# Neighbourhood attention of a two-layer hybrid encoder in twelve hand-ordered units, with the passage between layers and the first loads reordered

## The chip, the cores and the metric

The kernel runs on one core of a Trainium2 chip. A core has TensorE for matmuls (PE in the profile, its weight loads PEld), VectorE (DVE), ScalarE (ACT), GpSimd (POOL) and SyncE (SP, which here only issues DMA transfers). Each engine works through a queue of its own in a fixed order, and semaphores tie the queues together. The metric is the device time of one launch in microseconds (us), as the median of several runs. Less is better.

## The reference

Two layers over 512 tokens of width 1024, all in float32. The mixer of a layer projects the normalised input once, feeds three groups of heads from it, and adds the result to `x`; then a mixture of 16 experts follows, each of which takes its own best 64 tokens.

```python
def hybrid_layer(x, ...):
    hn = rms_norm(x, norm_mix)
    proj = jnp.einsum('bsd,dc->bsc', hn, w_in)               # 1024 -> 2336 columns
    qa, ka, va, cq, ckv, kr, hc, bc, cc = jnp.split(proj, splits, axis=-1)
    qa, ka = rms_norm(qa by heads, q_norm_a), rms_norm(ka by heads, k_norm_a)
    out_a = neighbourhood_attention(qa, ka, va, rpb)         # A: 6 heads of 64, 8 x 16 window on the 8 x 64 grid
    out_b = mla_attention(q, k, v)                           # B: 6 heads, q 96, v 64, all 512 keys
    out_c = short_conv_mixer(hc, bc, cc, conv_w)             # C: gated convolution of width 3, 256 channels
    mixed = concat(rms_norm(out_a), rms_norm(out_b), rms_norm(out_c))      # 384 + 384 + 256
    x = x + jnp.einsum('bsm,md->bsd', mixed, w_out)
    return x + expert_choice_moe(rms_norm(x, norm_ffn), ...)

def expert_choice_moe(x, ...):
    aff = jax.nn.softmax(x @ w_router + b_router)
    gate, idx = lax.top_k(aff.transpose(0, 2, 1), 64)        # each of 16 experts takes 64 tokens
    hid = silu(xs @ w_gate) * (xs @ w_up)                    # 1024 -> 1024
    ys = (hid @ w_down) * gate
    return zeros.at[idx].add(ys)
```

## The kernel before

Tokens lie on partitions in four blocks of 128 (`NJ` = 4). Matmuls that need float32 accuracy outside the experts are made of two rounded parts, `hi` and `lo`: `mm3` issues the three products hi·hi, lo·hi and hi·lo (its matmuls stand as L166, L167 and L168 in the profile, L178 to L180 after the change). ACT casts the hi part, and POOL or DVE subtracts it for the lo part.

The mixer has five stretches. `latents` loads the first weights by halves of a pair of row blocks (`wchunk`: a DMA, two casts L330 on ACT, two subtractions L331 on POOL), normalises `x` block by block (`norm_in`: Square L297, Ln and Exp L149/L151, a multiplication L300 on DVE, eight transposes L304 on PE, casts L309 and L310), and projects the latents of B (416 columns). `b_prep` and `conv` follow. Then `weave` drives `b_attn` step by step and slips steps of `a_prep`, the projection of A's q, k and v in 384-column pieces, between its steps as fills; `weave` drives `a_attn` in the same way, with loads of the output weights (`wo_loads`, L705, casts L712, subtractions L713) and the output products of C (`o1`, six 512-column matmuls a step) and B (`o2`, nine a step) as fills. The last, `o3`, multiplies A's own part after A's group norm (L381 to L389), and each output product is added to `x` on DVE (L726). In these stretches a scheduler orders each engine's queue from the written order and priorities (`first` gives the main generator a higher one).

`a_attn` goes over three pairs of heads and four query blocks. A head needs 64 rows of the array for its scores: 128 queries against 256 keys (outer blocks) or 384 keys (inner blocks). For each head: three score matmuls into a bank `sc`; the custom reduction TTR on DVE (L669: adds the bias, yields the negated maximum); Exp with its sum on ACT (L671); a reciprocal and a scaling on DVE (L673, L674); transposes into the bank `pt` (L677); a copy of these out of the bank (L679, on DVE for the first head of the pair and on ACT for the second); and the products with v (L685, 64 columns of the array each). The banks are four `prj`, two `sc`, one `pt` and one `po`.

The mixture of experts takes the experts in eight pairs. Its weights stream through nine slots of 2 MB, issued by SP (L892) in the order of use; the slots lie over the mixer's buffers, so the first loads wait until the mixer lets these go. A pair needs twelve loads of 2 MB. Matmuls of the experts are plain float32 (L158, `acc`). The last pair of a layer computes its two output halves one after the other and adds each with `scatter_rows` (cast and residue L958 and L959, products into `wk`, additions L965).

## Time and profile before

| | us |
|---|---|
| median of 3 runs | 1526.09 |
| lowest, highest | 1523.46, 1526.93 |
| the profiled execution | 1528.57 |
| its span | 1526.8 |

| engine | busy us | share of the span |
|---|---|---|
| PE | 1478.1 | 97% |
| PEld | 858.4 | 56% |
| DVE | 536.7 | 35% |
| ACT | 389.2 | 25% |
| POOL | 232.8 | 15% |

Durations are from the profiled execution; its time is 1.8 us over its span and 2.5 us over the median of the runs. The busy share of PE counts a matmul from its start to its modelled end, and neighbours overlap; the distance from one start to the next says more of what a matmul costs. PEclk in the tables by stretch is the granted TensorE clock, 1.00 for 2.4 GHz and 0.50 for 1.2 GHz. In time order: layer 0's mixer up to about 313 us, its experts up to 761 us, layer 1's mixer up to about 1070 us, its experts to the end.

### The profile page before, as it was taken

What the parts mean: (1) busy time and instruction counts of PE and PEld (TensorE: products, weight loads), DVE (VectorE), ACT (ScalarE), POOL (GpSimd) and SP (SyncE); (2) the same over time, 40 slices, a digit from 0 to 9 for tenths busy, and PEclk for the clock granted to TensorE, in tenths of its full rate; (3) what the DMA queues carried; (4) which work ended last, traced back from release to release, by engine and by line L of the source; (5) the groups of instructions that cost most, each with busy time, mean ns of one, the idle gap of its engine ahead of it and who ended that gap; (6) DMA issues with size and microseconds to landing.
All of it is one profiled execution on the core that took longest, in us unless ns stands there. A gap on an engine that the chain in (4) does not pass through costs nothing. (4 is left out here: it accounts for less than half of the span.)

```text
span 1526.8 us, 19989 instructions
## 1 busy us (share of the span) xinstructions
PE 1478.1 (97%) x8030; PEld 858.4 (56%) x8030; DVE 536.7 (35%) x1220; ACT 389.2 (25%) x969; POOL 232.8 (15%) x336
## 2 busy tenths in 40 slices
PE   7999999999999999999899999999999999999997
PEld 6877766645355355444288766666454554455342
DVE  5475456623023022112164654656130222123022
ACT  6465553400000000100164655543000000000001
POOL 3641360300000000000056314402000000000000
PEclk9999999999999999999999999899999999999999
DMA  5312131889999999999832122219899999999997
GB/s 171 88 46 61 30 111 56 340 315 425 420 427 426 428 427 427 428 428 426 351 89 73 50 55 62 70 56 403 311 422 428 427 428 427 428 427 428 426 429 302
DMA packets 58461, 441.72 MB, mean 289 GB/s; under 512 B 5633, under 2 KB 28161, under 8 KB 32769
## 3 DMA queue, kind: packets, MB, share of 16 engines
q1 hardware_dynamic: 56000, 437.04, 70.2%
q10 hardware_dynamic: 2368, 3.41, 0.8%
q8 instruction: 63, 1.03, 0.3%
q14 instruction: 30, 0.24, 0.0%
HBM read 438.33 MB, written 2.10 MB: 288 GB/s over the span
## 5 line engine op out<-in xcount | busy, mean ns | idle before, releaser
L158 PE MATMUL acc<-w,fmix 128*64 128x512 f32 x3072 | 671.8, 594 | 9.6 <-DMA w<-in_w_up_dram 5.0
L158 PEld LDWEIGHTS acc<-w,fmix 128*64 128x64 f32 x3072 | 215.9, 137 | 428.5 <-issue 407.3
L1001 DVE TENSOR_TENSOR tmp<-acc,tmp 128x512 f32<-128x512 f32 x32 | 22.1, 691 | 396.3 <-issue 368.4
L158 PEld LDWEIGHTS wk<-og,fmix 128*128 128x128 f32 x1024 | 121.0, 191 | 25.9 <-issue 22.7
L158 PE MATMUL wk<-og,fmix 128*128 128x128 f32 x1024 | 132.2, 279 | 0.7 <-DVE og L897 0.7
L995 POOL CAST sel<-con 16x128 bf16<-16x128 f32 x16 | 5.0, 316 | 768.0 <-PE wk L158 761.7
L331 POOL TENSOR_TENSOR wring<-fraw,wring 128x384 fp32r<-128x384 f32 (+1 forms) x88 | 91.2, 1045 | 142.0 <-ACT wring L330 136.7
L1000 ACT ACTIVATE tmp<-acc 128x512 f32<-128x512 f32 x32 | 19.0, 597 | 327.5 <-PE acc L158 327.5
L938 DVE SCALAR_TENSOR_TENSOR ys<-acc,stat,ys 128x256 fp32r<-128x256 f32 x56 | 26.8, 478 | 198.7 <-ACT ys L937 198.7
L937 ACT ACTIVATE ys<-acc,stat 128x256 fp32r<-128x256 f32 x56 | 26.6, 475 | 242.8 <-PE acc L158 191.7
L167 PE MATMUL prj<-wring,hn 128*128 128x384 f32 (+1 forms) x224 | 81.4, 363 | 0.0
L166 PE MATMUL prj<-wring,hn 128*128 128x384 f32 (+1 forms) x224 | 80.5, 361 | 0.3 <-ACT wring L330 0.3
L168 PE MATMUL prj<-wring,hn 128*128 128x384 f32 (+1 forms) x224 | 80.0, 357 | 0.1
L1010 ACT COPY fmix<-wk 128x512 f32<-128x512 f32 x32 | 17.4, 589 | 242.9 <-PE wk L161 242.9
L951 DVE TENSOR_TENSOR x<-wk,x 128x512 f32<-128x512 f32 x112 | 72.0, 684 | 2.2
L158 PE MATMUL wk<-ys,osc 128*128 128x256 f32 x448 | 63.8, 290 | 0.0
L907 DVE TENSOR_TENSOR fmix<-wk,pp 128x128 f32<-128x128 f32 (+1 forms) x86 | 30.7, 356 | 81.5 <-PE wk L158 81.5
L158 PEld LDWEIGHTS wk<-ys,osc 128*128 128x128 f32 x448 | 56.2, 191 | 0.0
L330 ACT CAST wring<-fraw 128x384 fp32r<-128x384 f32 (+1 forms) x88 | 44.5, 514 | 40.3 <-PE prj L167 15.7
L168 PEld LDWEIGHTS prj<-wring,hn 128*128 128x128 f32 x224 | 43.4, 194 | 5.4 <-issue 3.9
L166 PEld LDWEIGHTS prj<-wring,hn 128*128 128x128 f32 x224 | 43.6, 195 | 4.8 <-issue 3.0
L167 PEld LDWEIGHTS prj<-wring,hn 128*128 128x128 f32 x224 | 43.5, 194 | 5.0 <-issue 4.0
(272 smaller groups left out, 2004.6 us busy)
## 6 DMA issues: line engine op xcount, KB each, us to landing
w<-in_w_gate_dram SPq DMA_DIRECT2D x64, 2048.0 KB, 22.9
w<-in_w_up_dram SPq DMA_DIRECT2D x64, 2048.0 KB, 26.6
w<-in_w_down_dram SPq DMA_DIRECT2D x56, 2048.0 KB, 21.9
w<-in_w_down_dram SPq DMA_DIRECT2D x16, 1024.0 KB, 24.7
fraw<-in_w_in_dram SPq DMA_DIRECT2D x24, 384.0 KB, 3.2
fraw<-in_w_out_dram SPq DMA_DIRECT2D x16, 512.0 KB, 3.5
fraw<-in_w_in_dram SPq DMA_DIRECT2D x48, 128.0 KB, 2.4
fmix<-in_rpb_dram ACTq DMA_DIRECT2D x16, 144.0 KB, 3.4
```

Of the source, the lines that this page charges most:

```text
L158: return tc.keep_in_program_order(PE.matmul(*a, **k))
L166: PE.matmul(ps, ah, bh, start=first, stop=False)
L167: PE.matmul(ps, al, bh, start=False, stop=False)
L168: PE.matmul(ps, ah, bl, start=False, stop=last)
L330: ACT.copy(hi, raw[:, kk, :])
L331: POOL.tensor_tensor(lo, raw[:, kk, :], f(hi), op=OP.subtract)
L907: DVE.tensor_tensor(xsT[:, k0:k0 + nk, :], pg[:, 0:nk * 128].rearrange("p (k s) -> p k s", k=nk), P("gffn")[:, k0:k0 + nk, None].to_broadc ...
L937: ACT.activation(ys[:, 0:256], yq, AF.Copy, scale=gate)
L938: DVE.scalar_tensor_tensor(ys[:, 256:512], yq, gate, f(ys[:, 0:256]), op0=OP.mult, op1=OP.subtract)
L951: DVE.tensor_tensor(xv, po.rearrange("p (j c) -> p j c", j=2), xv, op=OP.add)
L1000: ACT.activation(hid, G[n], AF.Silu)
L1001: DVE.tensor_tensor(hid, U[n], hid, op=OP.mult)
```

## The change

Four places are edited.

1. A's attention. `a_attn` becomes `a_units`: twelve units (a pair of heads and a query block) of three parts, `scores`, `flips` and `output`, which the end of `mixer` calls in a written order: scores of the next unit, fills, transposes of this unit, fills, its products with v. The score matmuls of the two heads alternate. The matmuls of these parts, the softmax instructions, the copies out of the bank and the casts of the output weights are pinned to the written order (`PEo`, `ACTo`, `DVEo`, the last two from a new helper `Pinned`, whose instructions all stand under its line, L173). Both copies are on ACT now. The transposes go to `prj` banks, the probabilities to the seven buffers of `P`, the first output weights too; the output weights come in halves of 256 KB. B's group norm is woven in by steps. One of the twelve steps of `a_prep` moves from B's attention to A's, and the rest of `o2` from behind the last group norm's first matmul to before it.
2. First loads of layer 0. The norm weights come as one row and are spread over the partitions by two matmuls against ones and two ACT copies; of the constants the 128 columns of the identity come first, the rest after the weights; two of the four lo parts go from POOL to DVE; the normalisation runs one block ahead of the projection, no longer two.
3. Between the layers. `scatter_rows` works in 256-column quarters. Behind the first half's additions ACT sums the squares of that half of `x` into `half`, so that layer 1's `norm_in` squares only the other half and takes `half` as the bias of its Ln. `warm` issues matmuls on constants, two before and six after the second half's products.
4. At the end of the last layer the same quarters.

In the written-out orders below a row is one instruction or a run of equal ones, named by the line, the operation, what it writes and what it reads, and the shape. `sc` are scores, `prj` banks of projections and (after) transposes, `pt` transposes before, `po` the products with v, `P`, `tmf` and `tmp` probabilities and their transposes; `qk_103`, `qk_104` (`qk_102`, `qk_103` before) are A's q and k, `wring` and `hn` the operands of A's projection, `qk_106` and `lat` (`qk_105` and `lat` before) those of the output products.

PE in A's attention, before: the stretch with the second and third block of scores of the first pair of heads.

```order
L677 MATMUL pt<-con,tmf 128x128 x2
L167 MATMUL prj<-wring,hn_101 128x384
L168 MATMUL prj<-wring,hn_99 128x384
L166 MATMUL prj<-wring,hn_99 128x384
L167 MATMUL prj<-wring,hn_101 128x384
L168 MATMUL prj<-wring,hn_99 128x384
L166 MATMUL sc<-qk_103,qk_102 128x256
L167 MATMUL sc<-qk_103,qk_102 128x256
L168 MATMUL sc<-qk_103,qk_102 128x256
L166 MATMUL sc<-qk_103,qk_102 128x384
L166 MATMUL prj<-wring,hn_99 128x384
L167 MATMUL sc<-qk_103,qk_102 128x384
```

PE in A's attention, after: the third and fourth unit.

```order
L159 MATMUL sc<-qk_104,qk_103 128x256 x6
L162 MATMUL prj<-con,P 128x128 x6
L159 MATMUL prj<-qk_106,lat 128x512 x6
L159 MATMUL po<-tmp,fmix 64x128
L159 MATMUL po<-tmf,fmix 64x128
L159 MATMUL po<-tmp,fmix 64x128
L159 MATMUL po<-tmf,fmix 64x128
L159 MATMUL po<-tmp,fmix 64x128
L159 MATMUL po<-tmf,fmix 64x128
L159 MATMUL sc<-qk_104,qk_103 128x256 x6
L159 MATMUL prj<-qk_106,lat 128x512 x6
L162 MATMUL prj<-con,P 128x128 x4
```

Scores, transposes and products, which stood singly among the projection's matmuls, now stand in groups of four to six with the fills between the groups.

ACT in A's attention, before: exponentials (L671), copies of transposes (L679) and casts of output weights (L712) in the first pair of heads.

```order
L671 ACTIVATE tmf_2124,stat1_2127<-tmf_2124,stat1_2125 128x256
L671 ACTIVATE tmf_2147,stat1_2150<-tmf_2147,stat1_2148 128x384
L712 CAST hn0_98<-fraw_104 128x512
L679 COPY tmp_2135<-pt_2132 128x256
L712 CAST hn0_98<-fraw_104 128x512
L671 ACTIVATE tmf_2175,stat1_2178<-tmf_2175,stat1_2176 128x384
L712 CAST hn1_99<-fraw_104 128x512 x2
L671 ACTIVATE tmf_2199,stat1_2202<-tmf_2199,stat1_2200 128x384
```

ACT in A's attention, after: two units in the second pair of heads. The exponentials write `P`, the copies `tmp` and `tmf`.

```order
L173 ACTIVATE P_2324,stat1_2327<-P_2324,stat1_2325 128x256
L173 ACTIVATE P_2332,stat1_2335<-P_2332,stat1_2333 128x256
L173 CAST hn1_100<-fraw_105 128x512 x2
L173 COPY tmp_2357<-prj_2354 128x256
L173 COPY tmf_2362<-prj_2359 128x256
L173 COPY fmix_90<-po_2191 128x512
L173 ACTIVATE P_2381,stat1_2384<-P_2381,stat1_2382 128x384
L173 ACTIVATE P_2389,stat1_2392<-P_2389,stat1_2390 128x384
L173 COPY tmp_2408<-prj_2405 128x256
L173 COPY tmf_2413<-prj_2410 128x256
```

Both copies of a unit now stand behind both exponentials of the unit after it, and in this place also behind two casts of output weights.

ACT at the passage between the layers, before: residue casts (`yh`), layer 1's first weights (`qk2`, `wring`) and the norm of block 0 (`fmix` from `x`).

```order
L958 ACTIVATE yh_5155<-acc_5091,stat1_4989 128x256
L330 CAST qk2_5194<-fmix_89 128x416
L958 ACTIVATE yh_5155<-acc_5091,stat1_4989 128x256
L330 CAST qk2_5194<-fmix_89 128x416
L297 ACTIVATE fmix_89,stat1_5224<-x_67 128x1024
L330 CAST wring_5186<-fraw_5193 128x416
L149 ACTIVATE stat1_5226<-stat1_5224,eps_70 128x1
L330 CAST wring_5186<-fraw_5193 128x416
L151 ACTIVATE stat1_5228<-stat1_5226 128x1
```

ACT at the same place after.

```order
L1025 ACTIVATE ys_5182<-acc_5106,stat1_5004 128x256
L347 CAST qk2_5240<-fmix_90 128x416
L1025 ACTIVATE ys_5185<-acc_5106,stat1_5004 128x256
L347 CAST qk2_5240<-fmix_90 128x416
L311 ACTIVATE fmix_90,stat1_5270<-x_67 128x512
L150 ACTIVATE stat1_5272<-stat1_5270,half_82 128x1
L152 ACTIVATE stat1_5274<-stat1_5272 128x1
L311 ACTIVATE fmix_90,stat1_5292<-x_67 128x512
L347 CAST wring_5232<-fraw_5239 128x416 x4
```

The norm's square is half as wide, and its Ln and Exp stand ahead of the casts of `wring`; the first of two `qk2` casts still stands between the two residue casts.

The diff, cut:

```diff
+            return lambda *a, **k: tc.keep_in_program_order(getattr(self.eng, name)(*a, **k))
...
-        for g, _, _ in fills:
-            for _ in g:
-                pass
+        for g, _, w in fills:
+            if w < 5:
+                for _ in g:
+                    pass
...
-            ACT.activation(xn, x[:, j, :], AF.Square, scale=1.0 / 32.0, accum_out=ms)
-            r = rstd_of(ms, 1)
+            if l:
+                ACT.activation(xn[:, 512:1024], x[:, j, 512:1024], AF.Square, scale=1.0 / 32.0, accum_out=ms)
+                r = rstd_of(ms, 1, eps=half[:, j:j + 1])
...
+                    SP.dma_start(row, gm_in[l:l + 1, :])
+                    for n in range(2):
+                        c_ = slice(n * 512, (n + 1) * 512)
+                        ps = sc()
+                        PE.matmul(ps, ones[0:1, :], row[:, c_], start=True, stop=True)
+                        ACT.copy(gm[:, c_], ps)
...
-                SP.dma_start(con, con_in[:, 0:NCON])
+                SP.dma_start(con[:, 0:128], con_in[:, 0:128])
...
+                             None if kp < 2 else F(4992 + (kp - 2) * 832, 832), POOL if l or kp % 2 else DVE)
...
-            ahead = 2
+            ahead = 2 if l else 1
...
+                    pss = [sc(), sc()]
+                    for a, b in ((0, 0), (1, 0), (0, 1)):
+                        for hh in range(2):
+                            rows = slice(hh * 64, hh * 64 + 64)
+                            PEo.matmul(pss[hh][:, 0:n], qkA(0, a)[rows, hp, j * 128:(j + 1) * 128],
+                                       qkA(1, b)[rows, hp, k0 * 128:k1 * 128], start=a + b == 0, stop=b == 1)
...
+                        p = ptile()
...
+                        ACTo.activation(p[:, 0:n], p[:, 0:n], AF.Exp, bias=nm, scale=-1.0, accum_out=s_)
...
+                        pt = prj()
                         for i in range(k1 - k0):
-                            PE.transpose(pt[:, i * 128:(i + 1) * 128], p[:, i * 128:(i + 1) * 128], ident)
-                        pT = tmp()
-                        (ACT.copy if hh else DVE.tensor_copy)(pT[:, 0:n], pt[:, 0:n])
+                            PEo.transpose(pt[:, i * 128:(i + 1) * 128], ps_[hh][:, i * 128:(i + 1) * 128], ident)
+                        pT = (tmp, ftile)[hh]()
+                        ACTo.copy(pT[:, 0:n], pt[:, 0:n])
...
+                for a in {0: (0,), 1: (), 2: (1, 2)}.get(i, (i,)):
+                    if a < len(ks):
+                        raws.append([fraw(a % 2 * 1024 + n * 512, 512) if a else ptile() for n in range(2)])
+                        for n in range(2):
+                            SP.dma_start(raws[a][n], w_out[l, ks[a] * 128:(ks[a] + 1) * 128, n * 512:(n + 1) * 512])
...
+                        ACTo.copy(hi[:, c_], raws[i - 1][n])
...
+                    (DVEo if PE is PEo else DVE).tensor_tensor(x[:, j, c_], ps, x[:, j, c_], op=OP.add)
...
-        weave(b_attn(), 52, (ap, 1, 1), (norm_later(sc, oC, us[:, 0:512], 6, mixC), 1, 0),
-              (ap, 12 - 1, 1))
+        weave(b_attn(), 52, (ap, 1, 5), (norm_later(sc, oC, us[:, 0:512], 6, mixC), 1, 0), (ap, 11 - 1, 5))
...
-        weave(a_attn(), 40, (wl, 3, 0), (o1, 3, 4),
-              (norm_later(sc, oB, F(0, 512), 3, mixB), 1, 0), (wl, 1, 0), (o1, 5 - 3, 4), (wl, 1, 0), (o1, 4, 4),
-              (wl, 1, 0), (o2, 3, 3), (wl, 1, 0), (o2, 3, 3), (wl, 1, 0), (o2, 3, 3), (wl, 1, 0))
+        nb = norm_later(sc, oB, F(0, 512), 3, mixB, PEo, ACTo, DVEo)
+        todo = [(o1, 2), (nb, 1), (o1, 2), (wl, 0), (nb, 1), (o1, 2), (nb, 1), (o1, 2), (nb, 0), (wl, 0), (o1, 2),
+                (o1, 2), (wl, 0), (o1, 2), (o1, 2), (wl, 0)] + [(o2, 3)] * 3 + [(wl, 0)] + [(o2, 3)] * 3
+        todo += [(o2, 3)] * 2 + [(o1, 0), (o2, 0), (wl, 0)]
...
+        next(wl)
+        units[0][0]()
+        for _ in ap:
+            pass
+        next(wl)
+        units[1][0]()
+        next(wl)
+        for u, (_, flips, output) in enumerate(units):
+            if 0 < u < len(units) - 1:
+                units[u + 1][0]()
+            fill()
+            flips()
+            fill()
+            output()
+        tot = tmp()
+        squares(oA, tot)
+        place = places
+        fill()
+        for g, _ in todo:
+            next(g, None)
+        group_norm(sc, oA, tot, 0, mixA)
...
-            hi, lo = tmpr("yh"), tmpr("yl")
-            for q in range(2):
-                q_ = slice(q * 256, (q + 1) * 256)
-                ACT.activation(hi[:, q_], Y[n][:, q_], AF.Copy, scale=gate)
-                DVE.scalar_tensor_tensor(lo[:, q_], Y[n][:, q_], gate, f(hi[:, q_]), op0=OP.mult, op1=OP.subtract)
+            ys = [parts(Y, gate, 2 * n), parts(Y, gate, 2 * n + 1)]
             c_ = slice(n * 512, (n + 1) * 512)
+            between = l < layers - 1 and n
+            if between:
+                warm(2)
             for j in range(NJ):
                 po = wk()
-                PEo.matmul(po, osc[:, j * 128:(j + 1) * 128], hi, start=True, stop=False)
-                PEo.matmul(po, osc[:, j * 128:(j + 1) * 128], lo, start=False, stop=True)
+                for q in range(2):
+                    ps = po[:, q * 256:(q + 1) * 256]
+                    PEo.matmul(ps, osc[:, j * 128:(j + 1) * 128], ys[q][:, 0:256], start=True, stop=False)
+                    PEo.matmul(ps, osc[:, j * 128:(j + 1) * 128], ys[q][:, 256:512], start=False, stop=True)
                 DVE.tensor_tensor(x[:, j, c_], po, x[:, j, c_], op=OP.add)
+                if l < layers - 1 and n == 0:
+                    ACT.activation(po, x[:, j, c_], AF.Square, scale=1.0 / 32.0, accum_out=half[:, j:j + 1])
...
+        def warm(n):
+            po = wk()
+            for _ in range(n):
+                PEo.matmul(po, order[:, 2, :], order.rearrange("p a b -> p (a b)"), start=True, stop=True)
...
+                warm(6)
+                DVE.tensor_scalar(half, half, eps, None, op0=OP.add)
...
```

## Rows read from the trace of the kernel before

**Rows 1.** Busy time by stretch: us, each engine, granted clock, DMA.

```profile
core 0: us, PE busy (x) PEld busy (x) DVE busy (x) ACT busy (x) POOL busy (x), PEclk, DMA share, GB/s
110.00:188.40 78.40, 76.31 (x425) 55.09 (x425) 41.37 (x92) 45.09 (x114) 18.30 (x20) 0.98 0.16 44
188.40:267.80 79.40, 78.05 (x415) 51.87 (x416) 46.26 (x133) 36.79 (x90) 29.85 (x29) 1.00 0.23 80
942.10:1025.50 83.40, 82.21 (x415) 54.92 (x416) 45.85 (x133) 36.57 (x90) 29.85 (x29) 0.94 0.22 76
```

**Rows 2.** Waits of the queue on SP, whole span.

```profile
SPq L892 <- PE sc L168: 69.9, 2, 35.0
```

**Rows 3.** Chain that ended last, layer 1: start, us, engine, what.

```profile
1421.11 33.92 DMA w<-in_w_down_dram
1455.10 39.95 DMA w<-in_w_up_dram
```

**Rows 4.** PE in order of time, 191 us: start, us, line, what.

```profile
191.15 0.33 PE L166 MATMUL prj<-wring,hn 128*128 128x384 f32 x1
191.32 0.33 PE L167 MATMUL prj<-wring,hn 128*128 128x384 f32 x1
...
191.76 0.38 PE L166 MATMUL sc<-qk,qk 64*128 64x256 f32 x1
192.07 0.44 PE L166 MATMUL prj<-wring,hn 128*128 128x384 f32 x1
192.44 0.38 PE L167 MATMUL sc<-qk,qk 64*128 64x256 f32 x1
```

**Rows 5.** One head alone, then two, and their softmax, from 978 us.

```profile
978.63 0.38 PE L166 MATMUL sc<-qk,qk 64*128 64x256 f32 x1
...
979.17 0.50 PE L166 MATMUL prj<-qk,lat 128*128 128x512 f32 x1
...
979.39 0.42 DVE L669 CUSTOM_DVE_ANT_0 tmf<-sc,P 128x256 f32<-128x256 f32 x1 [0.82 <-PE sc L168]
...
979.86 0.51 ACT L671 ACTIVATE tmf<-tmf,stat 128x256 f32<-128x256 f32 x1
...
980.07 0.45 PE L166 MATMUL sc<-qk,qk 64*128 64x256 f32 x2
...
980.49 0.16 DVE L673 RECIPROCAL stat<-stat 128x1 f32<-128x1 f32 x1 [0.67 <-ACT tmf L671]
...
980.79 0.50 PE L166 MATMUL prj<-qk,lat 128*128 128x512 f32 x1
980.82 0.42 DVE L669 CUSTOM_DVE_ANT_0 tmf<-sc,P 128x256 f32<-128x256 f32 x1 [0.16 <-PE sc L168]
...
981.16 0.35 DVE L674 TENSOR_SCALAR tmf<-tmf,stat 128x256 f32<-128x256 f32 x1
```

**Rows 6.** ACT in A's attention, layer 0: groups, mean ns of one.

```profile
L671 ACT ACTIVATE tmf<-tmf,stat 128x384 f32<-128x384 f32 x12 | 7.4, 616 | 8.7 <-DVE stat L669 7.7 <-DVE tmf L674 0.8
...
L712 ACT CAST hn<-fraw 128x512 fp32r<-128x512 f32 x8 | 4.7, 619 | 2.4 <-DMA fraw<-in_w_out_dram 2.4
...
L679 ACT COPY tmp<-pt 128x256 f32<-128x256 f32 x6 | 2.2, 372 | 5.6 <-PE pt L677 5.6
```

**Rows 7.** DVE in the same stretch.

```profile
L726 DVE TENSOR_TENSOR x<-prj,x 128x512 f32<-128x512 f32 x13 | 8.9, 684 | 3.7 <-PE prj L168 3.7
...
L386 DVE SCALAR_TENSOR_TENSOR fmix<-fmix,pp,tmp 128x512 f32<-128x512 f32 x3 | 2.9, 953 | 0.0
L389 DVE TENSOR_TENSOR lat<-fmix,lat 128x512 fp32r<-128x512 f32 x3 | 2.7, 910 | 0.0
```

**Rows 8.** PE at the first projection of layer 0.

```profile
16.15 1.09 PE L304 MATMUL sc<-con,fmix 128*128 128x128 f32 x4 [4.55 <-DVE fmix L300]
```

**Rows 9.** All engines at the passage between the layers.

```profile
769.71 0.66 PE L304 MATMUL sc<-con,fmix 128*128 128x128 f32 x4 [2.29 <-DVE fmix L300]
...
771.95 0.70 PE L166 MATMUL prj<-wring,hn 128*128 128x416 f32 x1
```

More of the change, by code (lines that the diff above doesn't have):

```diff
@@ L125, in build @@
     gab = fix.tile([128, 2], F32, name="gab")
+    half = fix.tile([128, NJ], F32, name="half")
     def C(name):
@@ L163, in build, with __init__, __getattr__, mm3 @@
     PEo = Ordered()
-    def mm3(ps, ah, al, bh, bl, first, last):
+    class Pinned:
+        def __init__(self, eng):
+            self.eng = eng
+        def __getattr__(self, name):
+            return lambda *a, **k: tc.keep_in_program_order(getattr(self.eng, name)(*a, **k))
+    ACTo, DVEo, POOLo = Pinned(ACT), Pinned(DVE), Pinned(POOL)
+    def mm3(ps, ah, al, bh, bl, first, last, PE=PE):
         PE.matmul(ps, ah, bh, start=first, stop=False)
@@ L313, in mixer, with wchunk @@
         ring = [0]
-        def wchunk(kp, segs, n, home=None, raw=None):
+        def wchunk(kp, segs, n, home=None, raw=None, eng=POOL):
             i = ring[0] % 2
@@ L375, in squares, with group_norm, group_norm_steps @@
                 DVE.tensor_tensor(tot, tot, sq, op=OP.add)
-        def group_norm(bank, o, tot, k0, mix):
+        def group_norm(*args):
+            for _ in group_norm_steps(*args):
+                pass
+        def group_norm_steps(bank, o, tot, k0, mix, PE=PE, ACT=ACT, DVE=DVE):
             n = len(o)
@@ L637, in a_prep, with a_units, unit, scores @@
                 (ACT.copy if j % 2 else DVE.tensor_copy)(va[:, j, :], ps[j][:, 0:384])
-        def a_attn():
-            for hp in range(3):
-                bms = [{}, {}]
-                po = pob()
-                for j in range(NJ):
-                    k0, k1 = KEYS_OF[j]
-                    n = (k1 - k0) * 128
-                    pts = []
+        def a_units():
+            po, bms = [None], [{}, {}]
+            def unit(hp, j):
+                k0, k1 = KEYS_OF[j]
+                n = (k1 - k0) * 128
+                ps_, pts = [], []
+                def scores():
+                    if j == 0:
+                        bms[0], bms[1] = {}, {}
                     for hh in range(2):
                         h = 2 * hp + hh
-                        rows = slice(hh * 64, hh * 64 + 64)
                         if MASK_AT[j] not in bms[hh]:
@@ L684, in a_attn @@
                             h = 2 * hp + hh
-                            PE.matmul(po[hh * 64:hh * 64 + 64, j * 128:(j + 1) * 128],
-                                      va[:, k0 + i, h * DH:(h + 1) * DH], pts[hh][:, i * 128:(i + 1) * 128],
-                                      start=i == 0, stop=i == k1 - k0 - 1)
-                ACT.copy(oA[hp], po)
-            tot = tmp()
-            squares(oA, tot)
-            group_norm(sc, oA, tot, 0, mixA)
+                            PEo.matmul(po[0][hh * 64:hh * 64 + 64, j * 128:(j + 1) * 128],
+                                       va[:, k0 + i, h * DH:(h + 1) * DH], pts[hh][:, i * 128:(i + 1) * 128],
+                                       start=i == 0, stop=i == k1 - k0 - 1)
+                    if j == NJ - 1:
+                        ACTo.copy(oA[hp], po[0])
+                return scores, flips, output
+            return [unit(hp, j) for hp in range(3) for j in range(NJ)]
         mixs = mixA + mixB + mixC
```

74 lines of the change are left out of this document (44 added, 30 removed).

## The prediction

> **What bounds the kernel now.** I read the stretches first, then the chain and the waits of SP, then single instructions. In both stretches of A's attention, from the last product of B's attention to the first matmul of A's group norm, PE is busy for nearly the whole time while DVE, ACT and POOL each have a third of the time or more to spare: 78.05 of 79.40 us in layer 0, 82.21 of 83.40 us in layer 1 [rows 1]. So PE sets the length of these stretches today, and the question is what sets it after the change. Layer 1's stretch is 4.0 us longer for the same 415 matmuls, at a mean granted clock of 0.94 against 1.00; that is 12% of the stretch at 1.2 GHz.
>
> The experts' weights come as fast as DMA brings them: the chain that ended last runs through 33.92 and 39.95 us of transfers [rows 3]. Their first load waits for the last scores of A, 35.0 us of waiting in each of the two layers [rows 2], and the nine slots are full when the experts start. So what A's attention gains or loses shifts the whole rest of the layer, and I carry it to the end at its full size.
>
> **What PE would save.** A single matmul of 384 columns follows its like after 0.17 us (191.15 to 191.32). A projection matmul that stands between two score matmuls takes 0.37 us to the next start (192.07 to 192.44), and a score matmul 0.31 us (191.76 to 192.07) [rows 4]. So each change between 128 rows and 64 costs PE about 0.20 us. In the written order the changes per layer between the last product of B and A's group norm fall from 101 to 38: 63 x 0.20 = 12.6 us. The scores of one head take 0.54 us (978.63 to 979.17), those of two heads side by side 0.72 us (980.07 to 980.79) [rows 5]; two apart would take 1.08. Of the 0.36 us, 0.20 is a change that is already counted; with the wider inner blocks I estimate 0.25 us for each of twelve units, 3.0 us. PE alone would give back 15.6 us per layer, 31 us in all.
>
> **What the new order makes of it.** A unit now passes through a ring of waits. Scores of unit u+1; softmax of its first head and then of its second, since DVE holds the first head's reduction, reciprocal and scaling ahead of the second head's reduction; then, on ACT, the two copies of unit u, which stand behind both exponentials of u+1; then the products of u on PE, and only behind these the scores of u+2. For 256 keys, from the start of the scores: the first reduction at 0.75 us (980.07 to 980.82); its exponential 0.47 us later, its reciprocal at 1.10 us (979.39 to 979.86 and to 980.49), the scaling after 0.16 and for 0.35 us [rows 5]. So the second head's reduction starts 1.65 us behind the first, and its exponential ends at 0.75 + 1.65 + 0.47 + 0.51 = 3.4 us, read out by 3.5. Two copies of 0.372 us [rows 6] end at 4.25, the products after an estimated 0.55: 4.8 us. An inner unit's instructions are longer, 0.616 against 0.51 us for the exponential [rows 6], and in the same way comes to 5.9. With its mixed neighbours the mean of four units is 5.37 us. PE's own work for a unit is about 4.4 us: the stretch of 79.4, less 15.6, and with the moved matmuls below some 73 us, of which 16 lie before the loop and about 4 behind it, over twelve. PE would wait 1 us in every unit. The ring, not PE, then sets the stretch, and this is where the saving goes.
>
> The sum of the stretch, for one layer: 88 projection matmuls of 384 columns x 0.173 and the first scores, 16.0 us until the scores of unit 1. Ten turns of the ring, 53.7 us. In two places a pair of weight casts of 0.62 us [rows 6] stands between the exponentials and the copies: 2.5 us. B's group norm puts 0.95 and 0.91 us [rows 7] on DVE ahead of the next reduction in three units; DVE has some 1.2 us free there, so 0.7 each, 2.1 us. From the last scores: softmax 4.2, the copies and products of two units 3.9, their transposes 0.75, the bank's copy, a square and an addition 1.9, about 10.8 us. Together 85.1 us.
>
> Of the 88 projection matmuls 27 lay before this stretch, in B's attention. PE is busy for 76.31 of 78.40 us there [rows 1], so I credit their 4.7 us in full; the least would be nothing, if B's softmax chain sets that stretch once the cover is thinner. That gives 80.4 us against 79.4 and 83.4: +1.0 in layer 0 and -3.0 in layer 1, whose slow clock I take as gone because the alternating scores before it are. Bounds: -15.6 in each layer if PE still sets the stretch; +4.7 if the credit fails, and beyond that see the third rival.
>
> The 20 matmuls of 512 columns that lay behind the group norm's first matmul (4.6 us, at 0.23) now stand before it. I give nothing for them: the products of A wait for Ln, Exp, 0.95 us of scaling and 0.91 us of residue behind that matmul in any case, and two weight casts (1.24 us) stand ahead of the Ln on ACT. Bounds -4.6 and +1.2.
>
> A rule of the Trainium skill speaks against the change. The reciprocal at 980.49 ends 0.67 us of idle time of DVE, spent on an exponential [rows 5], so DVE waited at the head of its queue. The page TensorE: Matmul & The Clock Gate (its table of specifications) says that ScalarE and VectorE take their queue strictly in order and that only TensorE may pull weight loads forward. By it the ready copies wait behind the exponentials and a unit takes 5.37 us; could ACT take them first, it would be PE's 4.4 us. The trace agrees as far as it shows one such wait.
>
> **The first loads.** Before, PE waits 4.55 us for the second block's norm, whose transposes stand in front of the first block's remaining matmuls [rows 8]. One block ahead, this wait goes, but the projection then runs into its weight parts, which ACT and POOL turn out one by one, and a short gap of about 1.2 us opens behind each of two or three later sets of transposes. Net -1.5 us; bounds -4.5 (all of the wait) and +2 (gaps without the gain). The two broadcasting matmuls and copies lie where PE and ACT wait for the weights.
>
> **The passage.** Block 0's square is half as wide and two weight casts leave the way of its Ln, so I estimate its transposes, at 769.71 before [rows 9], some 1.9 us earlier. But its cast to `hn` now stands behind five weight casts on ACT, and POOL has yet to make their residues; of the 1.9 us the first projection matmul, at 771.95 [rows 9], keeps 0.5. The six warming matmuls fill PE's gap; that first matmul lasts 0.70 us [rows 9], against 0.33 for one of 384 columns [rows 4], and if it and the five behind it start 0.17 us closer, as at 2.4 GHz, this is another 1.0 us. Together -1.5 us; bounds -3 and +1.
>
> **The tail.** The first products of the last half start on one quarter instead of two: about 0.1 us, and in the first halves of both layers 0.2 each: -0.5 us, bounds -1 and 0.
>
> Sum: 1.0 - 3.0 - 1.5 - 1.5 - 0.5 = -5.5 us. Against the profiled execution's 1528.57 us this gives 1523.1; that execution lay 2.5 us over the median, so on the median 1526.09 - 5.5 = 1520.6 us.
>
> **Rivals.** (a) PE still sets the stretch. For it: 98% today. Against it: the order of copies behind exponentials. It gives 2 x -15.6 on A, -3.5 on the rest: 1491 us. (b) Half of it, because the scheduled parts overlap better than my ring (the second head's reduction earlier, products behind one copy): 0.6 us less per unit, 11 units, two layers, -13: 1507 us. (c) Slower, by DVE's pinned queue. The additions to `x` (0.684 us [rows 7], five for three units) stand behind the second head's scaling and ahead of the next unit's first reduction, and each waits for a fill that PE issues late. DVE's own chain in a unit, two softmax halves of 1.65 and 1.14 us of additions behind a reduction at 0.75, ends at 5.2 us, against a need at 5.37 + 0.75. The slack is 0.9 us. From the point where an addition's matmuls end later than that, every turn of the ring grows; at 0.9 us a turn, 22 turns, it is +20 us on my sum: 1540 us. (d) The loads hide everything after the passage, and only layer 0's start and the tail count: 1524 us.
>
> **How the numbers follow.** The forecast has 0.42 and spreads over -10 to +4 around it, (a) 0.11, (b) 0.20, (c) 0.22, (d) 0.05. What a measurement of this kernel tells from no change is 0.2%, 3.05 us: below 1523.0 counts as faster, above 1529.1 as slower. Faster: 0.11 + 0.20 + 0.6 x 0.42 = 0.56. Slower: 0.22 + 0.08 x 0.42 = 0.25. Same: the rest, 0.19. The range runs from 1500, below which lies (a), to 1538, near the middle of (c); it leaves out about 0.2. The likeliest case's own range is 1511 to 1525.
>
> **What would show it.** In the profile after: turns of 4.8 to 5.9 us from scores to scores, with PE idle for about 1 us in each, released by ACT's copies; exponentials before copies with no gap between them; 80 to 81 us from the last product of B to A's group norm, once the 4.7 us shorter stretch of B's attention is taken in; granted clock 1.00 there; no wait of 4.55 us before layer 0's second transposes; the first projection of layer 1 about 1.5 us earlier behind the last expert. The forecast is wrong if PE is busy through the loop, if PE's waits end with an addition or a reduction on DVE, or if the clock falls to 1.2 GHz for whole units.

## The result: slower by 1.4%, and the profile after

| | before | after |
|---|---|---|
| median of 3 runs, us | 1526.09 | 1547.88 |
| lowest, highest, us | 1523.46, 1526.93 | 1545.87, 1548.43 |
| span of the profiled execution, us | 1526.8 | 1546.6 |

After to before is 1.0139, 95% interval 1.0122 to 1.0156. The forecast was 1520.6 us, the range 1500 to 1538: the change went the other way and out of the range.

Where the 19.9 us between the two spans lie, by the starts of the same instructions in both traces (us):

| stretch | layer 0 before | after | layer 1 before | after |
|---|---|---|---|---|
| start (layer 1: last expert matmul) to B's first scores | 97.3 | 98.8 | 92.2 | 90.6 |
| to B's last product | 90.7 | 89.2 | 89.2 | 88.5 |
| to the matmul of A's group norm | 79.9 | 94.0 | 83.9 | 94.0 |
| to the first expert matmul | 47.0 | 47.0 | 47.0 | 46.9 |
| the experts | 445.5 | 444.5 | 445.4 | 444.1 |

The loss is A's attention, some 14 and 10 us, and it reaches the end nearly undiminished: the experts take only about 1 us less each than they took. Busy time by stretch, after, for A's two stretches:

```profile
188.00:282.00 94.00, 81.11 (x467) 61.99 (x463) 43.72 (x124) 42.30 (x107) 34.20 (x35) 0.89 0.18 62
952.60:1046.70 94.10, 81.20 (x467) 61.95 (x463) 43.83 (x124) 42.31 (x107) 34.24 (x35) 0.89 0.17 62
```

Against [rows 1] PE has gone from 98% busy to 86%, and the granted clock from 1.00 and 0.94 to 0.89. Inside the stretch, layer 0's loop in three parts: the first turn of the ring (scores of unit 1 to scores of unit 2), turns 2 to 5, and turns 6 to 10:

```profile
204.50:217.08 12.58, 8.79 (x35) 5.01 (x34) 4.82 (x11) 5.94 (x13) 5.66 (x5) 0.73 0.13 42
217.08:244.44 27.36, 21.91 (x116) 16.30 (x114) 15.13 (x44) 13.39 (x34) 10.17 (x10) 0.75 0.12 40
244.44:271.50 27.06, 23.80 (x163) 17.53 (x161) 15.12 (x47) 12.62 (x35) 12.20 (x14) 1.00 0.12 40
```

The last five turns take 27.06 us, 5.41 each; 5.37 was forecast. One by one they take 5.85, 5.05, 4.62, 5.33 and 6.20 us, where 4.8 was forecast for an outer and 5.9 for an inner unit. The first five take 39.94 us.

The first turn, on ACT, POOL and PE (start, us, line, what, idle before and what ended it):

```profile
205.01 1.14 ACT L173 CAST qk<-P 128x512 fp32r<-128x512 f32 x2
206.07 0.61 ACT L173 ACTIVATE P<-P,stat 128x384 f32<-128x384 f32 x1
...
208.95 0.61 ACT L173 ACTIVATE P<-P,stat 128x384 f32<-128x384 f32 x1 [2.17 <-DVE stat L173]
...
209.56 1.12 ACT L173 CAST qk<-fraw 128x512 fp32r<-128x512 f32 x2
```

```profile
210.24 2.50 POOL L766 TENSOR_TENSOR qk<-fraw,qk 128x512 fp32r<-128x512 f32 x2 [2.02 <-ACT qk L173]
```

```profile
207.05 0.50 PE L159 MATMUL prj<-qk,lat 128*128 128x512 f32 x1 [0.63 <-POOL qk L766]
210.22 2.15 PE L159 MATMUL prj<-qk,lat 128*128 128x512 f32 x3 [2.67 <-ACT qk L173]
212.16 1.05 PE L162 MATMUL prj<-con,P 128*128 128x128 f32 x4
```

The casts of C's second block of output weights (209.56) stand behind unit 1's exponentials. The first fill on PE needs them, and unit 0's transposes, ready since 204, wait behind that fill until 212.16.

The second turn: PE's transposes and products, and ACT.

```profile
217.80 0.87 PE L162 MATMUL prj<-con,P 128*128 128x128 f32 x6
218.43 1.62 PE L159 MATMUL prj<-qk,lat 128*128 128x512 f32 x6
222.58 0.69 PE L159 MATMUL po<-tmp,fmix 128*64 128x128 f32 x2 [2.52 <-ACT tmp L173]
```

```profile
219.58 0.61 ACT L173 ACTIVATE P<-P,stat 128x384 f32<-128x384 f32 x1 [1.83 <-DVE stat L173]
...
221.45 0.61 ACT L173 ACTIVATE P<-P,stat 128x384 f32<-128x384 f32 x1 [1.16 <-DVE stat L173]
...
222.07 0.46 ACT L173 COPY tmp<-prj 128x384 f32<-128x384 f32 x1
```

The transposes are done before 218.7, but ACT, idle for 1.83 and 1.16 us, copies them only from 222.07, behind both exponentials of the next unit; PE idles 2.52 us for them. This is the ring as it was forecast. The Trainium skill (TensorE: Matmul & The Clock Gate, table of specifications) gives ScalarE a strict first-in, first-out queue; the trace agrees: the transposes lie ready for 3.4 us. The ring is longer than forecast because the exponentials are late, and the reason stands on DVE:

```profile
216.35 0.75 DVE L173 SCALAR_TENSOR_TENSOR fmix<-fmix,pp 128x512 f32<-128x512 f32 x1 [3.25 <-ACT fmix L173]
217.78 0.69 DVE L173 TENSOR_TENSOR lat<-fmix,lat 128x512 fp32r<-128x512 f32 x1 [0.69 <-ACT lat L173]
218.39 0.68 DVE L173 TENSOR_TENSOR x<-prj,x 128x512 f32<-128x512 f32 x1
218.99 0.55 DVE L173 CUSTOM_DVE_ANT_0 P<-sc,P 128x384 f32<-128x384 f32 x1
```

Unit 2's scores began at 217.08. Its reduction (218.99) comes 1.9 us later, not 0.75, because a step of B's group norm is pinned ahead of it and itself waits for a cast on ACT; behind that step also stands an addition to `x`.

In layer 0's first projection PE now waits three times for parts of the weights, and then runs at the lower clock (the last row: 0.51). The 4.55 us of [rows 8] are gone, but the last matmul of the projection starts at 42.4 us, against 40.9 before:

```profile
14.46 0.45 PE L178 MATMUL prj<-qk,hn 128*128 128x416 f32 x1 [0.90 <-ACT qk L347]
15.61 0.46 PE L180 MATMUL prj<-qk,hn 128*128 128x416 f32 x1 [0.50 <-POOL qk L348]
17.61 0.72 PE L180 MATMUL prj<-qk,hn 128*128 128x416 f32 x1 [1.16 <-POOL qk L348]
```

```profile
17.80:24.40 6.60, 6.58 (x22) 5.56 (x23) 4.44 (x13) 3.93 (x15) 0.91 (x4) 0.51 0.25 59
```

At the passage the rows that answer to [rows 9] come 8.6 and 10.4 us behind the last expert matmul (773.50), before 9.4 and 11.7 (760.29):

```profile
782.10 1.09 PE L321 MATMUL sc<-con,fmix 128*128 128x128 f32 x8
...
783.90 0.46 PE L178 MATMUL prj<-wring,hn 128*128 128x416 f32 x1 [0.71 <-ACT hn L326]
```

### The profile page after: what moved, and what is told of

Read it like the earlier page. It is cut to its first block, busy times and chain, and to the rows that moved or that the text cites. A ratio compares the mean times of both kernels' runs of the same rounds, so it can differ in the third digit from the quotient of the medians.

```text
span 1546.6 us, 20129 instructions
## 1 busy us (share of the span) xinstructions
PE 1473.1 (95%) x8074; PEld 865.2 (56%) x8074; DVE 529.8 (34%) x1201; ACT 397.4 (26%) x1003; POOL 225.3 (15%) x332
## 3 DMA queue, kind: packets, MB, share of 16 engines
q8 instruction: 64, 1.05, 0.3%
## 5 line engine op out<-in xcount | busy, mean ns | idle before, releaser
L159 PEld LDWEIGHTS wk<-og,fmix 128*128 128x128 f32 x1024 | 121.0, 191 | 25.9 <-issue 22.7
L1026 DVE SCALAR_TENSOR_TENSOR ys<-acc,stat,ys 128x256 fp32r<-128x256 f32 x64 | 30.7, 480 | 227.8 <-ACT ys L1025 227.8
L1025 ACT ACTIVATE ys<-acc,stat 128x256 fp32r<-128x256 f32 x64 | 30.4, 475 | 269.2 <-PE acc L159 216.4
L178 PE MATMUL prj<-wring,hn 128*128 128x384 f32 (+1 forms) x224 | 79.3, 355 | 1.6 <-ACT hn L326 1.6
L159 PE MATMUL wk<-ys,osc 128*128 128x256 f32 x512 | 76.0, 293 | 4.5 <-ACT ys L1025 2.9
L179 PE MATMUL prj<-wring,hn 128*128 128x384 f32 (+1 forms) x224 | 79.2, 354 | 0.6 <-DVE hn L327 0.5
L180 PE MATMUL prj<-wring,hn 128*128 128x384 f32 (+1 forms) x224 | 78.5, 351 | 0.0
L159 PEld LDWEIGHTS wk<-ys,osc 128*128 128x128 f32 x512 | 65.1, 191 | 10.0 <-ACT ys L1025 7.3
L347 ACT CAST wring<-fraw 128x384 fp32r<-128x384 f32 (+1 forms) x88 | 44.7, 514 | 43.8 <-PE prj L179 18.0
L178 PEld LDWEIGHTS prj<-wring,hn 128*128 128x128 f32 x224 | 43.3, 194 | 5.0 <-ACT hn L326 2.5
L180 PEld LDWEIGHTS prj<-wring,hn 128*128 128x128 f32 x224 | 42.9, 191 | 4.9 <-issue 4.3
L173 ACT ACTIVATE P<-P,stat 128x256 f32<-128x256 f32 (+1 forms) x48 | 27.0, 562 | 72.1 <-DVE stat L173 70.0
```

The source lines that it names most:

```text
L159: return tc.keep_in_program_order(PE.matmul(*a, **k))
L173: return lambda *a, **k: tc.keep_in_program_order(getattr(self.eng, name)(*a, **k))
L178: PE.matmul(ps, ah, bh, start=first, stop=False)
L179: PE.matmul(ps, al, bh, start=False, stop=False)
L180: PE.matmul(ps, ah, bl, start=False, stop=last)
L347: ACT.copy(hi, raw[:, kk, :])
```

## Experiments

Theory 1: what is pinned into the ring from other stages (C's weight casts, B's group norm) makes the first turns long. Theory 2: the copies behind both exponentials make every turn long. Rivals: the loss comes from the first loads or the passage; the missing step in B's attention. The kernel before was timed again beside each group of experiments, at medians of 1524.3 to 1525.2 us, so the ratios to it are compared, each with its 95% interval. The changed kernel has 1.0139, and a point is 1% of before, 15.3 us.

**e1: A's attention, its weaving and loads as before, the rest changed.**

```diff
...
-        units = a_units()
+        weave(a_attn(), 40, (wl, 3, 0), (o1, 3, 4),
+              (norm_later(sc, oB, F(0, 512), 3, mixB), 1, 0), (wl, 1, 0), (o1, 5 - 3, 4), (wl, 1, 0), (o1, 4, 4),
...
```

> The changed first loads, passage between the layers and tail, but A's attention, its weaving and the output weights' loads as before. Theory (the loss lies in A's attention alone): the two traces give +1.4 us at the end of layer 0's first projection, -1.6 us at layer 1's, about -1 us in each layer's experts, so 1523 to 1527 us, against 1526.1 before and 1547.9 after. Rival (the other three edits carry a good part of the loss, by way of what they move in the schedule): over 1533 us.

1524.52 us, ratio 0.9996 (0.9984 to 1.0009). The whole loss lies in A's attention and what is woven into it; first loads, passage and tail together are worth nothing. That nothing is a sum: in this run's trace the first projection's last matmul starts at 44.7 us, 3.8 later than before, and layer 1's attention, unchanged, takes 80.3 us at a granted clock of 1.00, where it took 83.9 at 0.94.

**e2: two blocks ahead in layer 0.**

```diff
-            ahead = 2 if l else 1
+            ahead = 2
```

> The changed kernel with layer 0's normalisation two blocks ahead of the projection again, as before; all else as changed. Theory: the one-block lead is what made layer 0's first projection end at 42.4 us instead of 40.9, by leaving PE waits of 0.9, 0.5 and 1.2 us before 18 us, after which the granted clock falls to 0.50 until 24 us: the projection ends at 40 to 41 us, 1.5 to 2.5 us less in all, 1545.5 to 1546.4. Rival (the lead is not what matters; the weights' residues on POOL and DVE are): within 0.5 us of 1547.9.

1539.09 us, ratio 1.0095 (1.0068 to 1.0123): 0.44 points, about three times what was expected. The last matmul of layer 0's first projection starts at 36.1 us instead of 42.4. PE has one wait of over a microsecond there, of 1.29 us, and no stretch at the lower clock behind it:

```profile
14.85 1.07 PE L321 MATMUL sc<-con,fmix 128*128 128x128 f32 x8 [1.29 <-DVE fmix L317]
```

```profile
16.00:20.00 4.00, 4.00 (x26) 3.93 (x25) 3.86 (x15) 3.80 (x17) 1.33 (x3) 1.00 0.94 253
```

The rest of the edit to the first loads is a gain of 4.9 us against before; the lead of one block took it away again. How much it took varies: in e3 to e6 and e9, which keep the lead of one block, that matmul starts at 41.1 to 41.7 us, with 2 to 5 us at the lower clock behind the first waits instead of 6.8.

**e3: group norm of B and C's casts ahead of the loop.**

```diff
-        todo = [(o1, 2), (nb, 1), (o1, 2), (wl, 0), (nb, 1), ...
+        todo = [(o1, 2), (o1, 2), (wl, 0), (o1, 2), (o1, 2), (wl, 0), (o1, 2),
...
         units[0][0]()
+        next(wl)
+        next(wl)
+        for _ in nb:
+            pass
         for _ in ap:
             pass
-        next(wl)
         units[1][0]()
-        next(wl)
```

> The changed kernel, with B's group norm and the casts of the output weights of C moved from the first turns of the loop to the stretch of A's projection ahead of it; order of copies and exponentials unchanged. Theory 1 (the excess of the first turns comes from work for other stages that is pinned into the ring: weights' casts behind exponentials, which hold up the first fill, and the group norm's steps on DVE ahead of a reduction; waits of over 2 us on PE there are followed by stretches at the lower clock): turns 1 to 6, now 12.5, 7.4, 6.0, 6.9, 7.2 and 5.8 us, fall to 5 to 6 each, some 8 to 11 us a layer: 1526 to 1532 us. Theory 2 (the copies behind both exponentials are the bulk): at most 3 us a layer, 1542 us or more.

1569.34 us, ratio 1.0301 (1.0283 to 1.0320): a miss. The first turn did fall, from 12.5 to 5.3 us, but the stretch ahead of it grew from 4.9 to 20.3: PE waited 10.83 us for two casts of A's last projection weights. These waited for their load, and the load for POOL's residues of C's weights, which, cast early, still held its buffer (12.7 us of waiting on SP):

```profile
207.46 0.38 SPq L340 DMA_DIRECT2D fraw<-in_w_in_dram  x1
210.72 0.92 ACT L347 CAST wring<-fraw 128x384 fp32r<-128x384 f32 x2 [3.75 <-DMA fraw<-in_w_in_dram]
211.28 0.69 PE L178 MATMUL prj<-wring,hn 128*128 128x384 f32 x1 [10.83 <-ACT wring L347]
```

The work had only been put in front of something else. It does not tell the theories apart in time. Moved this far forward, the steps also change what the kernel computes, so this run speaks of times and waits alone.

**e4: copies between the next unit's two exponentials.** `scores` is split into its matmuls with the first head's softmax, and the second head's softmax.

```diff
...
-            if 0 < u < len(units) - 1:
-                units[u + 1][0]()
-            fill()
+            ahead_ = 0 < u < len(units) - 1
+            if ahead_:
+                units[u + 1][0](0)
             flips()
+            if ahead_:
+                units[u + 1][0](1)
+            fill()
             fill()
             output()
```

> The changed kernel, with a unit's two copies on ACT between the next unit's first and second exponential instead of behind both; for that the transposes follow the scores at once and both fills come after them. Group norm and weights' casts stay where they are. Theory 2 (copies behind both exponentials set every turn): the copies come about 1 us earlier, every turn falls by 0.6 to 1.0 us as far as PE's own 4.4 us lets it, 7 to 10 us a layer: 1528 to 1534 us. Theory 1 (the first six turns are set by what is pinned into them from other stages): turns 7 to 11 gain 0.5 each, the first ones little, 2 to 4 us a layer: 1540 to 1544 us.

1528.70 us, ratio 1.0034 (1.0022 to 1.0045): 1.05 points, within what theory 2 expected. Turns 6 to 10 fall from 27.1 to 22.5 us. In turn 7 both copies stand between the exponentials, and the products follow 3.43 us behind the scores (243.63), where in the changed kernel they come 3.87 us behind (254.16 and 250.29). First e4, then the changed kernel:

```profile
245.36 0.51 ACT L173 ACTIVATE P<-P,stat 128x256 f32<-128x256 f32 x1 [1.25 <-DVE stat L173]
...
245.87 0.46 ACT L173 COPY tmp<-prj 128x384 f32<-128x384 f32 x1
...
246.23 0.48 ACT L173 COPY tmf<-prj 128x384 f32<-128x384 f32 x1
...
247.06 0.32 PE L159 MATMUL po<-tmp,fmix 128*64 128x128 f32 x1
...
247.35 0.51 ACT L173 ACTIVATE P<-P,stat 128x256 f32<-128x256 f32 x1 [0.64 <-DVE stat L173]
```

```profile
253.14 0.51 ACT L173 ACTIVATE P<-P,stat 128x256 f32<-128x256 f32 x1 [1.02 <-DVE stat L173]
...
253.65 0.46 ACT L173 COPY tmp<-prj 128x384 f32<-128x384 f32 x1
254.00 0.48 ACT L173 COPY tmf<-prj 128x384 f32<-128x384 f32 x1
...
254.16 0.43 PE L159 MATMUL po<-tmp,fmix 128*64 128x128 f32 x2 [0.38 <-ACT tmp L173]
```

The first turn stays at 12.2 us, so theory 1 holds beside theory 2. The fills moved behind the transposes in the same edit, and in most turns the two are not separated. In turn 7 PE's order is the same in both kernels (scores, transposes, nine matmuls of fills, products), so there it is not the place of the fills that takes the turn from 5.05 to 4.23 us.

**e5: C's second block cast ahead of unit 1's exponentials.**

```diff
         next(wl)
+        next(wl)
         units[1][0]()
-        next(wl)
```

> The changed kernel with one step moved: the casts of the second block of C's output weights (two on ACT, two residues on POOL) stand ahead of unit 1's exponentials instead of behind them. Theory 1 (the first turn of 12.5 us is set by these casts, since the first fill on PE waits for them and the transposes wait behind the fill): casts end at about 3 us after unit 1's scores instead of 6, POOL's four residues follow each other and end some 2 us earlier; with less of the lower clock behind, 2 to 4 us a layer: 1540 to 1544 us. Theory 2 (the ring of copies and exponentials alone): no change or 1 us more a layer, since unit 1's exponentials come 1.2 us later, 1548 to 1550 us.

1540.29 us, ratio 1.0096 (1.0078 to 1.0114): 0.43 points. The first turn falls from 12.5 to 8.8 us in both layers, twice 3.7 us. The casts now start at 204.16 us, 1.5 behind unit 1's scores instead of 5.0, and what the first fill still waits for is POOL's residue of them:

```profile
204.16 1.14 ACT L173 CAST qk<-fraw 128x512 fp32r<-128x512 f32 x2
...
207.74 0.50 PE L159 MATMUL prj<-qk,lat 128*128 128x512 f32 x1 [1.62 <-POOL qk L766]
```

**e6: all twelve steps of A's projection in B's attention.**

```diff
-        weave(b_attn(), 52, ..., (ap, 11 - 1, 5))
+        weave(b_attn(), 52, ..., (ap, 12 - 1, 5))
```

> The changed kernel with all twelve steps of A's projection woven into B's attention as before (eleven there now). Theory (B's attention no longer keeps PE busy once the last step is gone, so that the 27 matmuls cost next to nothing there): the stretch from B's first scores to its last product grows by at most 1.5 us, and A's falls by 4.7: 3 us a layer less, 1540 to 1543 us. Rival (PE sets both stretches, the credit in the prediction was right and is given back): within 1.5 us of 1547.9.

1548.27 us, ratio 1.0147 (1.0128 to 1.0165): no gain. In layer 0 the stretch of B grows by 2.9 us, and the first turn takes 15.4 us, so that the matmul of A's group norm comes 183.3 us behind B's first scores, as it did (183.2). In the first turn the fill still waits for the casts of C's second block, until 210.66 us, where it was 210.22: the time taken from ahead of the loop is waited for inside it. Whether the credit of 4.7 us would hold without that wait stays open.

**e7: A's attention as before, two blocks ahead** (e1 with the edit of e2).

```diff
-            ahead = 2 if l else 1
+            ahead = 2
```

> A's attention as before, the other edits as changed, but two blocks ahead in layer 0's normalisation. Theory (the lead alone spoils the first loads, the broadcast, the split constants and DVE's residues are a gain): layer 0's first projection ends some 5 us earlier than before (36 against 40.9 us), which comes out at the end: 1518 to 1521 us, against 1524.5 with the lead of one block. Rival (the gain seen with the new A's attention was chance of that run): 1523 to 1526.

1516.39 us, ratio 0.9945 (0.9929 to 0.9962), 0.51 points below e1. The rival is out: the lead does the same with the old attention.

**e8: copies between the exponentials from the first turn on, casts early, first fill a step of the group norm, two blocks ahead.** The edits of e2, e4 and e5, with the loop's condition opened for unit 0, and

```diff
-        todo = [(o1, 2), (nb, 1), (o1, 2), (wl, 0), (nb, 1), ...
+        todo = [(nb, 1), (o1, 2), (o1, 2), (wl, 0), (nb, 1), ...
```

> The changed kernel with three of the edits together: copies between the exponentials in every turn, the first included; C's weight casts ahead of unit 1's exponentials, with the first step of B's group norm as the first fill; two blocks ahead in layer 0. Theory 1 and 2 both hold: -19 for the copies, -9 for the lead, -4 to -10 for the first turns: 1510 to 1520 us, below before's 1524 to 1526. If the first turns stay at 12 us whatever stands in them (DVE's pinned queue): 1520 us or more.

1515.63 us, ratio 0.9944 (0.9928 to 0.9961). It beats before, but not e7: the new attention is now as long as the old one (80.1 and 80.4 us, in e7 80.0). The first turn falls to 7.5 us, but turns 1 to 4 still take 26.0 us in layer 0; unit 3's reduction comes 4.9 us behind its scores.

**e9: B's group norm not pinned, all else as changed.**

```diff
-        nb = norm_later(sc, oB, F(0, 512), 3, mixB, PEo, ACTo, DVEo)
+        nb = norm_later(sc, oB, F(0, 512), 3, mixB)
```

> The changed kernel with B's group norm woven in at the same places but not pinned: the scheduler puts its steps where it likes on PE, ACT and DVE; all else as changed. Theory 1, its second half (the group norm's scaling and residue, pinned on DVE between a unit's scaling and the next unit's first reduction, wait for casts on ACT and hold up reductions until 1.4 to 1.9 us after the scores instead of 0.8): reductions of units 2 to 5 come 0.6 to 1.1 us earlier, turns 2 to 5, 27.4 us together, fall to 23 to 25, 2.5 to 4.5 us a layer: 1539 to 1543 us. Rival (DVE has room there; the waits have the copies behind them alone): within 1.5 us of 1547.9.

1539.93 us, ratio 1.0095 (1.0072 to 1.0117): 0.44 points. Reductions of units 2 to 4 come 0.92, 0.77 and 0.77 us behind their scores (1.92, 1.41 and 1.54 before the edit); turns 2 to 5 fall from 27.4 to 22.7 us in layer 0. Unit 2's scores start at 216.30 us there:

```profile
215.82 0.69 DVE L173 TENSOR_TENSOR x<-prj,x 128x512 f32<-128x512 f32 x1 [0.30 <-PE prj L159]
216.43 0.68 DVE L410 TENSOR_TENSOR lat<-fmix,lat 128x512 fp32r<-128x512 f32 x1
217.22 0.56 DVE L173 CUSTOM_DVE_ANT_0 P<-sc,P 128x384 f32<-128x384 f32 x1
```

**e10: e8 with the edit of e9.**

> The kernel of the three edits together (copies between the exponentials, C's casts ahead of unit 1's exponentials, two blocks ahead; 1515.6 us) with B's group norm not pinned as well. Theory: its reductions of units 2 to 4 come 2.6, 4.9 and 3.3 us after their scores, where 1.2 would do, since the group norm's steps stand in front of them on DVE; turns 1 to 4, 26 us together, fall to 20 to 23: 3 to 6 us a layer, 1504 to 1510 us. Rival (PE then waits for something else at once, such as the weights' residues): 1513 us or more.

1508.82 us, ratio 0.9899 (0.9872 to 0.9925), within what was expected. Turns 1 to 4 take 21.0 us.

**e11: e10, and C's first block cast ahead of the copies of v.**

```diff
         units[0][0](1)
+        next(wl)
         for _ in ap:
             pass
         next(wl)
-        next(wl)
```

> As the run before, and the first block of C's weights is cast ahead of the copies of v, so that POOL's residues start some 2 us earlier. Theory (the first turn still waits for POOL's four residues of 1.28 us each): the first turn falls by 1 to 1.5 us, 2 to 3 us in all below the run before. Rival (the copies of v that are now later hold up the first products): no difference or 1 us more.

1504.72 us, ratio 0.9863 (0.9840 to 0.9886): faster than before by 1.4%, and than the changed kernel by 2.8 points. Its interval overlaps that of e10; in the traces the first turn falls from 7.5 to 6.0 us and A's stretch from 75.3 to 73.2 us in each layer. The loop, from the scores of unit 1 to those of unit 11:

```profile
198.10:244.50 46.40, 44.84 (x306) 32.34 (x305) 32.71 (x98) 29.72 (x79) 27.41 (x28) 1.00 0.18 58
```

46.4 us for what took 67.0, PE busy for 97% of it at full clock. PE sets the stretch again: A's stretch takes 73.2 us in both layers, and "some 73 us" was the prediction's figure for PE's own work. So its saving on PE comes out as a whole; no run changes the order of the matmuls alone, so what the fewer changes of rows and columns give of it is not shown. The four single edits (e2, e4, e5 and e9) give 0.44, 1.05, 0.43 and 0.44 points, 2.36 in all; e10, which has them all, the opened first turn and the other first fill, has 2.40. They add up within their intervals: none of them gains what another also gains. The three in A's attention, 1.92 points, are more than the 1.39 that were lost.

## Why the prediction was wrong

By the spans, 25 us lie between the forecast -5.5 and the measured +19.9. A's stretch has 17 of them: 85.1 us were forecast with the moved matmuls in it, 94.0 came in each layer. B's stretch has 7, the first loads 3; the experts gave back 2.

The mechanism that was to eat the saving was named and is shown: the ring through ACT's copies, at 5.41 us a turn where 5.37 was forecast, and e4 took 1.05 points from it. The ends of the stretch were right too: the scores of unit 1 come 16.5 us behind B's last product (16.0), A's group norm 10.5 us behind the last scores (10.8). That layer 1's slow clock of before would go was wrong, new stretches took its place, and one of the prediction's own signs of being wrong came: in turns 3 and 5 the granted clock is 0.62. What failed:

1. The terms for what else stands in the ring. "In two places a pair of weight casts ...: 2.5 us" and the group norm's 2.1 us were added as durations, 4.6 us. The first five turns took 39.9 us where the ring alone makes some 27: 13 us, some 2 of them the lower clock (last section). These were waits in a chain, and were priced as work. In the first turn, 7 us longer than the ring, a cast of 1.2 us behind unit 1's exponentials held up the fill on PE and the transposes behind the fill; moving it took 3.7 us (e5), and the other edits around it brought the turn to 7.5 us (e8) and, with the first block cast earlier too, to 6.0 (e11). A step of the group norm on DVE waits for ACT, and the reduction behind it waits with it. e5 and e9 measure the two at 0.43 and 0.44 points, together 6.7 us a layer.
2. "I credit their 4.7 us in full", of the 27 projection matmuls that left B's attention: B's stretch fell by 1.5 and 0.7 us only, and in the other runs the same eleven steps take 88.4 to 90.5 us, so that even this is not sure. PE was 97% busy there, but not with work that could be taken away for its own length. With the lower bound that the prediction named, nothing, its sum would have been 4.7 us a layer higher.
3. The first loads were to give -1.5 us and gave +1.4. The gaps for the weight parts came about as forecast, 2.6 us in all, but the wait of 4.55 us does not need the lead of one block to go: with two blocks ahead 1.29 us of it are left (e2), and the projection's last matmul starts 6.3 us earlier. e2 and e7 show that two blocks are the better order by 0.44 and 0.51 points.
4. The tail's 0.1 us did not come (8.9 us from the last expert matmul to the end in both). The 0.2 us of each first half cannot be told apart within the 1 us that each of the experts' stretches lost.

The passage was right in its sum, -1.6 us for -1.5, but by luck: the transposes came 0.8 us earlier (1.9 forecast), the first matmul 1.3 (0.5), and what followed gave 0.3 (1.0).

The 101 and 38 changes that the prediction counted are of rows and of columns together; 62 and 24 of them are between 128 rows and 64. Its price of 0.20 us is read from changes of rows. In the trace before, a change of columns costs about as much: a 512-column matmul behind products of 64 columns takes 0.34 us to the next start, 0.23 among its like.

The third rival, DVE's pinned queue, had the place right and the wrong instructions. In the changed kernel the additions to `x` hold up no reduction by themselves: in e9 they are still pinned, and the reductions of units 2 to 4 come 0.77 to 0.92 us behind the scores. In e4, where the turns are shorter, two additions do stand ahead of unit 7's reduction, which comes at 1.21 us instead of 0.76. The rival's time, 1540 us, came nearest of all, but from another cause.

## What to carry to other kernels

When an order is written by hand for several engines, follow each engine's queue and ask of every instruction what it waits for and who stands behind it; an instruction that belongs to another stage is to be priced by the wait that it brings, not by its duration. Pin the chain that matters and leave the rest to the scheduler: one unpinned group norm gave 0.44 points. A stretch in which PE is 97% busy need not shorten by all the PE work that leaves it: here 4.7 us left, and 1.5 and 0.7 were gained.

## What the runs showed of the hardware

Waits of PE can be followed by stretches at 1.2 GHz. In layer 0's loop after the change waits of 2.67, 2.52 and 2.93 us end at 210.2, 222.6 and 236.0 us, and the granted clock around them is:

```profile
208.80:215.70 6.90, 5.35 (x12) 3.25 (x13) 1.39 (x5) 3.19 (x8) 3.15 (x3) 0.53 0.24 76
215.70:222.60 6.90, 4.38 (x31) 2.95 (x29) 3.95 (x11) 3.09 (x8) 0.66 (x1) 0.97 0.00 0
222.60:229.50 6.90, 6.90 (x32) 5.31 (x32) 4.47 (x13) 3.75 (x10) 5.08 (x5) 0.54 0.22 77
235.90:242.70 6.80, 6.72 (x26) 5.17 (x27) 2.25 (x9) 2.88 (x10) 1.81 (x2) 0.50 0.24 77
```

They need not be. In layer 0 of e5 PE waits as long in turns 2 to 4, and the clock stays at 1.00; in layer 1 of the same run it falls. Turns 2 to 5, first layer 0, then layer 1, and layer 0's waits:

```profile
211.44:236.80 25.36, 16.70 (x118) 12.04 (x116) 14.84 (x44) 12.84 (x34) 9.28 (x10) 1.00 0.15 43
968.64:996.11 27.47, 21.72 (x116) 16.21 (x114) 15.39 (x44) 13.39 (x34) 10.13 (x10) 0.75 0.12 39
```

```profile
217.19 0.43 PE L159 MATMUL po<-tmp,fmix 128*64 128x128 f32 x2 [2.77 <-ACT tmp L173]
223.85 0.43 PE L159 MATMUL po<-tmp,fmix 128*64 128x128 f32 x2 [2.67 <-ACT tmp L173]
230.60 0.43 PE L159 MATMUL po<-tmp,fmix 128*64 128x128 f32 x2 [2.93 <-ACT tmp L173]
```

The same order takes 25.4 us at full clock and 27.5 at 0.75. So of what turns 2 to 5 lose in the changed kernel (27.4 us at 0.75) the clock has some 2 us, as an estimate; at full clock, too, they are 4 us longer than four turns of the ring. Why the clock fell in one layer and not in the other stays open.

A DVE instruction took longer while POOL worked: the scaling of 384 columns 1.43 us at 207.01, during POOL's residues from 205.71 to 208.2, and 0.42 us at 209.89, when POOL had nothing to do until 210.24. It stands in the chain of the first turn, ahead of unit 1's second exponential and so of C's casts, and adds 1 us there. That POOL is the cause was not tested.
